# Hybrid attention/convolution layer: places of their own for the first head's weight pieces, loads issued in order of need, sums of squares on VectorE

## The chip, the cores and the metric

The kernel runs on one NeuronCore of a Trainium2 chip. The metric is the device time in microseconds of one execution. Three timed runs of the kernel before gave a median of 2090.63 us (2089.04 to 2090.69). One further execution was profiled; it took 2091.11 us, and the profile covers a span of 2087.8 us of it. All places in time below (for instance "44.2 us") count from the start of that span.

## The reference, cut to what matters

One decoder layer on 512 tokens of width 2048, preceded by 16 meta tokens (528 columns in all), in float32:

```python
n = _rmsnorm(h, g_mix[l])                    # h: 528 x 2048
p = n @ w_in[l]                              # 2048 x 6144: q, k, v, b, c, u
q = _rmsnorm(q.reshape(b, L, 8, 128), g_q)   # 8 heads of 128
k = _rmsnorm(k.reshape(b, L, 8, 128), g_k)
o_attn = _stick_breaking_attention(q, k, v)
o_conv = gb * _causal_dwconv(gc * u, conv_w[l])
o = concat(_rmsnorm(o_attn), _rmsnorm(o_conv))
h = h + o @ w_out[l]
n2 = _rmsnorm(h, g_ffn[l])
h = h + (silu(n2 @ w_gate) * (n2 @ w_up)) @ w_down
```

The root mean square of a token needs all 2048 features of x. The kernel does not wait for it: it multiplies x by the gain only, runs the projections on that, and applies the token's scale `r` to their results.

## The kernel before, in words

Features lie on the 128 partitions, tokens on the free axis. x is 16 tiles `xt` of 128 features by 528 tokens; a weight matrix comes in pieces of 128 rows by a few hundred to 1024 columns. Each operand of a product is split into two parts of a 32-bit matmul type: `hi` (a cast on ScalarE) and `lo` (the rest, a subtraction on VectorE). A tile then takes three matmul passes, hi by hi, hi by lo and lo by hi, on lines 276, 278 and 280 (`product_steps`).

**Stages.** First the eight heads: for each head a product for k, one for q and one for v (`pk`, `pq`, `pv`, 16 tiles each), with the attention of the head before interleaved. Then two convolution channel groups by plain products (`pcu`, `pb`), six by a scheme that needs seven block products for eight (lines 732 to 734), then the output projection, and the feed-forward layer, which fills most of the time.

**The first head** is where the change lies. Its k and q products are built alongside the loading and splitting of x. The list `FIRST` cuts the 16 tiles into groups of 2, 2, 4, 4 and 4. For each group there is one weight piece for k and one for q: ten pieces, four of 256 columns and six of 512. They are the loads 0 to 9; the loads 10 and 11 are the two pieces of v (1024 columns each). For a group the code loads its x tiles (`load_x`, line 341), splits them (`split_x`), runs the group's k and q tiles (`next(step)`), and squares its x tiles (`square_x`). `split_x` makes `nh` (line 348 on ScalarE for the first four tiles and the even ones, line 350 on GpSimd for the odd ones from the fifth) and `nl` (line 351, VectorE). `square_x` writes squares on ScalarE (line 359) and adds them on line 360, for even tiles on GpSimd and for odd tiles on VectorE, into two accumulators.

**Places of the weights.** All raw weights pass through one buffer, `w_buf`, with four places of 1024 columns (`PLACES`). `load_at` issues the next load of the list on SyncE's queue (line 173). When a piece has been split (lines 189 and 190), `done_with` issues the next load into the place that it leaves. So the fifth load waits for the first split, and so on. The split pieces go into `s_buf`, which has three places; splits run two pieces ahead of the product. SyncE's queue works in order: behind a load that waits for a place, the loads of x wait too.

**Order of the other work.** `after(n, work)` registers work that runs n tiles later in the program (`tick`). `x_scale` (line 326: it adds the two accumulators, sums over partitions by a matmul on line 330, and makes `r` and `eps_r2`) is registered 8 tiles before the end of the first head's q product. The norms of k and q (`qk_norm`, its `finish` part) run 8 and 10 tiles into the v product; `attend` starts 11 tiles into the next head's k product. `form_blocks(k)` prepares operands for the later convolution products: it loads four pieces of x (line 413), combines them on VectorE, splits them and stores them to the tensor `fc` (line 422). `form_blocks(0)` to `(6)` run in heads 1 to 7, `form_blocks(7)` at the start of the convolution; line 691 reads `fc` back.

The program is laid out by a planner that keeps the written order where operands are expected to be ready and lets other ready work go ahead where they are not; each engine then runs its own list in order, and waits on semaphores.

Of the kernel before, what the change touches and what calls it, by code (L numbers as in the profile page):

```python
# [10 lines left out]
F32R = mybir.dt.float32r  # L11
AF = mybir.ActivationFunctionType
ALU = mybir.AluOpType
PSUM = bass.MemoryType.PSUM

P = 128
D = 2048
SEQ = 512
META = 16
L = META + SEQ  # L20
HEADS = 8
FF = 5632
KT = D // P
# [10 lines left out]
def hybrid_layer(ctx: ExitStack, tc: tile.TileContext, xT, w_in, w_out, w_gu, w_down, vecs, out):  # L34
# [9 lines left out]
    nc = tc.nc  # L44
    ve, sc, gp, pe = nc.vector, nc.scalar, nc.gpsimd, nc.tensor
# [9 lines left out]
    const = open_pool("const", side="right")  # L55
# [13 lines left out]


    vec = keep.tile([P, 75], F32, name="vec")
    gp.dma_start(vec, vecs)
    sc.preload_act_table_set("natural_log_exp_and_others")
    g_mix, g_ffn = vec[:, 0:16], vec[:, 16:32]
    g_att, g_cnv = vec[:, 32:40], vec[:, 40:48]
# [15 lines left out]
        channel_multiplier=1,  # L91
    )

    carry = const.tile([P, P], F32R, name="carry")
    ve.tensor_copy(carry, later)
    ve.tensor_copy(carry[0:1, :], ones[0:1, :])
    ones_r = keep.tile([P, P], F32R, name="ones_r")
    ve.tensor_copy(ones_r, ones)
    later_r = const.tile([P, P], F32R, name="later_r")
    ve.tensor_copy(later_r, later)  # L100
    gq_s = const.tile([P, 1], F32, name="gq_s")
    ve.tensor_scalar(gq_s, g_q, 1.0 / math.sqrt(P), None, ALU.mult)

# [49 lines left out]
    for n in CHUNKS[1:]:  # L153
        for j in range(KT // 2):
            plan_pair(n, [w_down[2 * j + m, k][:, k0 * P : (k0 + n) * P] for k in range(2) for m in range(2)])
        k0 += n

    quads, sums, split_w, used, loaded = {}, {}, [], [0], [0]

    sixth = next(n for n, (i, _) in enumerate(ents) if i != "raw" and pairs[i][0] == 6)  # L160
# [4 lines left out]
    SUMS = {8: (4096, 5120), 6: (3840, 4608)}  # L165
    n_sums = [1]

    def load_at(place):
        key, n, w = loads[loaded[0]]
        loaded[0] += 1  # L170
        t = w_buf[:, place : place + n * P]
        quads[key] = t, place, n
        nc.sync.dma_start(t.rearrange("p (t c) -> p t c", t=2) if len(w.shape) == 3 else t, w)

    def done_with(key):
        _, place, n = quads[key]
        if loaded[0] < len(loads):
            for p in MOVED[place] if loads[loaded[0]][1] == 6 != n else (place,):
                load_at(p)

# [75 lines left out]
    def after(k_tiles, work):  # L256
        waiting.append([k_tiles, work])
# [60 lines left out]
    H = L // 2  # L318
# [20 lines left out]
    def load_x(k):  # L339
        xts.append(xpool.tile([P, L], F32, tag="xt", name=f"xt{k}"))  # L340
        nc.sync.dma_start(xts[k], xT[k])
# [12 lines left out]
    def square_x(k):  # L354
        if k < 2:
            sc.activation(accs[k], xts[k], AF.Square)
        else:
            s = t512(L, "r", 3)
            sc.activation(s, xts[k], AF.Square)
            (gp, ve)[k % 2].tensor_tensor(accs[k % 2], accs[k % 2], s, ALU.add)  # L360

    pk0 = pp.tile([P, 2, 512], F32, tag="pp", name="pk0")
    pq0 = pp.tile([P, 2, 512], F32, tag="pp", name="pq0")
# [1 line left out]
        product_steps([(pk0[:, 0, :H], 0, H), (pk0[:, 1, :H], H, L)], n_hl, KT),  # L365
        product_steps([(pq0[:, 0, :], META, L)], n_hl, KT),
    ]
    load_at(PLACES[0])
    load_x(0)
    load_at(PLACES[1])  # L370
    for a, b in FIRST:
        for k in range(len(xts), b):
            load_x(k)
        if not a:
            load_at(PLACES[2])
            load_at(PLACES[3])
        for k in range(a, b):
            split_x(k)
        if b == KT:
            for k in range(a, b):  # L380
                square_x(k)
            after(8, x_scale)
        for step in steps:
            next(step)
        if b < KT:
            for k in range(a, b):
                square_x(k)
    xpool.release()


# [17 lines left out]
    def form_blocks(k):  # L408

        x4 = stage.tile([P, 4, CH], F32, tag="x4", name=f"x4_{k}")  # L410
        st = stage.tile([P, 8 * CH], F32R, tag="st", name=f"st4_{k}").rearrange("p (i a t) -> p i a t", i=4, a=2)
        for i, kk in ((0, k), (2, k + 8)):
            nc.sync.dma_start(x4[:, i : i + 2], two(xT[kk][:, C0:]))
        for i, kk in ((0, k), (2, k + 8)):
            sc.activation(x4[:, i : i + 2], x4[:, i : i + 2], AF.Copy, scale=g_mix[:, kk : kk + 1])
        a11, a21, a12, a22 = (x4[:, i] for i in range(4))
        ve.tensor_tensor(a22, a22, a21, ALU.subtract)
        ve.tensor_tensor(a21, a11, a21, ALU.subtract)
        ve.scalar_tensor_tensor(a11, a22, -1.0, a11, ALU.mult, ALU.subtract)
        ve.scalar_tensor_tensor(a12, a11, -1.0, a12, ALU.mult, ALU.subtract)  # L420
        split(st[:, :, 0], st[:, :, 1], x4)
        nc.sync.dma_start(fc[:, :, :, k].bitcast(F32), st.bitcast(F32))
# [11 lines left out]
    def halves(ps, n):  # L434
        return ps[:, :, :n]
# [4 lines left out]
    def qk_norm(ps, g, cols, dst, parts_of, name):  # L440

        raw = t512(L, "e", 2)[:, :cols]
        s = t512(L, "e2", 2)[:, :cols]
        sh = apool.tile([P, L], F32R, tag="sh", name=f"sh_{name}")[:, :cols]
        sl = apool.tile([P, L], F32R, tag="sl", name=f"sl_{name}")[:, :cols]
        cuts = [(0, cols)] if cols == SEQ else [(0, H), (H, L)]
        raw_v, s_v = (raw, s) if cols == SEQ else (two(raw), two(s))  # L450
        sc.activation(s_v, ps, AF.Square)
        sc.activation(raw_v, ps, AF.Copy, scale=g)
        split(sh, sl, s)

        def finish():
            v = t512(L, "v", 2)[:, :cols]
            for a, b in cuts:
                q = small(f"ss_{name}{a}")[:, : b - a]
                pe.matmul(q, ones_r, sh[:, a:b], start=True, stop=False)
                pe.matmul(q, ones_r, sl[:, a:b], start=False, stop=True)  # L460
                ve.scalar_tensor_tensor(
                    v[:, a:b], q, 1.0 / P, eps_r2[:, L - cols + a : L - cols + b], ALU.mult, ALU.add
                )
            y = t512(L, "e2", 2)[:, :cols]
            rsqrt(y, v, cols)
            ve.tensor_tensor(dst, raw, y, ALU.mult)
            hi, lo, n = parts_of
            split(hi, lo, dst[:, :n])

        return finish  # L470
# [3 lines left out]
    def head(h):  # L474

        if h:
            pk = pp.tile([P, 2, 512], F32, tag="pp", name=f"pk{h}")
            product([(pk[:, 0, :H], 0, H), (pk[:, 1, :H], H, L)], n_hl)
        else:
            pk = pk0  # L480
        kn = kns[0]
        kh = apool.tile([P, 384], F32R, tag="kh", name=f"kh{h}")
        kl = apool.tile([P, 384], F32R, tag="kl", name=f"kl{h}")
        after(8, qk_norm(halves(pk, H), g_k, L, kn[:, :L], (kh, kl, 384), f"k{h}"))

        if h:
            pq = pp.tile([P, 2, 512], F32, tag="pp", name=f"pq{h}")
            product([(pq[:, 0, :], META, L)], n_hl)
        else:
            pq = pq0  # L490
        qn = apool.tile([P, SEQ], F32, tag="qn", name=f"qn{h}")
        qh = apool.tile([P, SEQ], F32R, tag="qh", name=f"qh{h}")
        ql = apool.tile([P, SEQ], F32R, tag="ql", name=f"ql{h}")
        after(9 if h else 10, qk_norm(pq[:, 0, :], gq_s, SEQ, qn, (qh, ql, SEQ), f"q{h}"))

        pv = pp.tile([P, 2, 512], F32, tag="pp", name=f"pv{h}")
        product([(pv[:, 0, :H], 0, H), (pv[:, 1, :H], H, L)], n_hl)
        vt = t512(L, "e", 2)
        ve.tensor_tensor(two(vt[:, :L]), halves(pv, H), two(r), ALU.mult)
        after(6 if h else 11, lambda: attend(h, kn, kh, kl, qn, qh, ql, vt))  # L500
# [117 lines left out]
        after(14, lambda: sums(2))  # L618

    for h in range(HEADS):  # L620
        if h:
            after(6, lambda h=h: form_blocks(h - 1))
        head(h)

    def token_scale(acc, dst, count, name, work, eng=ve):
# [40 lines left out]

    for j in range(CONV_FIRST):
        if j == 0:
            after(2, lambda: form_blocks(7))
        c1, c2 = halves_of("e"), halves_of("e2")  # L670
        for c in (c1, c2):
            p = pp.tile([P, 2, 512], F32, tag="pp", name="pcu")
            product([(p[:, 0, :CH], C0, C0 + CH), (p[:, 1, :CH], C0 + CH, L)], n_hl)
            sc.copy(two(c), halves(p, CH))
        y = t512(SEQ, "v", 2)[:, :SEQ]
        conv_taps(j, two(c1), two(c2), y)
        pb = pp.tile([P, 2, 512], F32, tag="pp", name=f"pb{j}")
        product([(pb[:, 0, :], META, L)], n_hl)
        gb = t512(SEQ, "e2", 2)[:, :SEQ]
        sc.copy(gb, pb[:, 0, :])  # L680
        if j == 0:
            assert not waiting
            after(10, scale_a)
            apool.release()
            atmp.release()
            const.release()
            blk_pool = open_pool("blk_pool", side="right")
            blk = blk_pool.tile([P, 3, 2, 8, CH], F32R, name="blk")
            for i, n in ((2, 3), (0, 0), (1, 2)):
                for part in range(2):  # L690
                    gp.dma_start(blk[:, i, part], fc[:, n, part], max_dma_last_dim=4160)
        oh, ol, store = stage_out(f"c{j}")
        conv_out(j, gb, y, oh, ol, t512(SEQ, "e", 2)[:, :SEQ], ve)
        store()
# [493 lines left out]
```

## Time and profile before

| what | number |
|---|---|
| median of three runs | 2090.63 us |
| profiled execution, span of its profile | 2091.11 us, 2087.8 us |
| TensorE busy, share of the span | 2046.0 us, 98% |
| VectorE, ScalarE, GpSimd busy | 1723.3, 1046.5, 414.9 us |
| mean granted TensorE clock | 0.991 |
| first head's k and q on TensorE | from 5.4 to 44.2 us |

In the profile PE is TensorE, DVE VectorE, ACT ScalarE, POOL GpSimd and SP SyncE; a q behind an engine is its queue, in which DMAs are issued and waits are held. A row of the timeline gives a start, a duration, the engine, the line of the kernel, the operation, the tile written and the tiles read, a count, and in brackets the idle time of the engine just before, with what ended it. "xN" merges N neighbouring instructions, so a merged row's duration includes what lies between them. A row of the view by windows gives a stretch, its length, each engine's busy time with its count of instructions, the granted clock of TensorE, the busy share of the 16 DMA engines, and the rate at which they moved data. A row of a group gives line, engine, operation, tiles, shapes and count, then busy time and mean ns of one, then the idle time before them.

### The profile page before, as it was taken

What the parts mean: (1) busy time and instruction counts of PE and PEld (TensorE: products, weight loads), DVE (VectorE), ACT (ScalarE), POOL (GpSimd) and SP (SyncE); (2) the same over time, 40 slices, a digit from 0 to 9 for tenths busy, and PEclk for the clock granted to TensorE, in tenths of its full rate; (3) what the DMA queues carried; (4) which work ended last, traced back from release to release, by engine and by line L of the source; (5) the groups of instructions that cost most, each with busy time, mean ns of one, the idle gap of its engine ahead of it and who ended that gap; (6) DMA issues with size and microseconds to landing.
All of it is one profiled execution on the core that took longest, in us unless ns stands there. A gap on an engine that the chain in (4) does not pass through costs nothing.

```text
span 2087.8 us, 39731 instructions
## 1 busy us (share of the span) xinstructions
PE 2046.0 (98%) x16158; PEld 1979.0 (95%) x16158; DVE 1723.3 (83%) x2186; ACT 1046.5 (50%) x1511; POOL 414.9 (20%) x559
## 2 busy tenths in 40 slices
PE   8999999999999998999999999999999889999999
PEld 6999999999998888999999999999999889999999
DVE  7878877578877778998989989989899867888887
ACT  5666656444443435554555555545555433444443
POOL 3111111220015443111110111111101332223110
PEclk8999999999999999999999999999999989999999
DMA  6343334653356656556554555655555989989864
GB/s 205 107 152 118 121 123 133 219 154 106 103 205 186 183 177 217 153 175 175 163 162 149 169 154 148 173 155 162 164 150 172 300 239 237 262 233 252 242 155 86
DMA packets 161686, 362.21 MB, mean 173 GB/s; under 512 B 13456, under 2 KB 73360, under 8 KB 161504
## 3 DMA queue, kind: packets, MB, share of 16 engines
q1 hardware_dynamic: 78368, 225.80, 34.3%
q0 software_dynamic: 83136, 133.89, 24.4%
q8 instruction: 126, 2.06, 0.4%
q14 instruction: 56, 0.46, 0.1%
HBM read 278.76 MB, written 80.87 MB: 172 GB/s over the span
## 4 chain that ended last, share of the span: by engine, by line
PE 88%; DMA 3%; DVE 3%; issue 2%; ACT 1%; POOL 1%; SPq 0%; DVEq 0%; POOLq 0%; ACTq 0%
PE x L732 12%; PE x L734 12%; PE x L733 12%; PE z L732 6%; PE z L733 6%; PE z L734 6%; PE y L733 3%; PE y L732 3%; PE y L734 3%; PE po L829 3%; PE po L830 3%; PE po L831 3%; PE pv L276 1%; PE pv L278 1%; PE pv L280 1%
## 5 line engine op out<-in xcount | busy, mean ns | idle before, releaser
L189 ACT CAST s_buf<-w_buf 128x1024 fp32r<-128x1024 f32 (+2 forms) x665 | 659.4, 992 | 790.4 <-PE x L733 350.6
L190 DVE TENSOR_TENSOR s_buf<-w_buf,s_buf 128x1024 fp32r<-128x1024 f32 (+2 forms) x665 | 769.8, 1158 | 197.8 <-ACT s_buf L189 196.7
L733 PE MATMUL x<-f,s_buf 128*128 128x256 f32 x1408 | 388.3, 276 | 3.0 <-DMA f<-fx 1.8
L734 PE MATMUL x<-f,s_buf 128*128 128x256 f32 x1408 | 388.1, 276 | 3.0 <-DVE s_buf L190 3.0
L732 PE MATMUL x<-f,s_buf 128*128 128x256 f32 x1408 | 388.1, 276 | 0.2 <-ACT f L290 0.2
L198 DVE TENSOR_TENSOR w_buf<-w_buf 128x1024 f32<-128x1024 f32 (+1 forms) x243 | 278.5, 1146 | 19.0 <-DMA w_buf<-w_in 10.7
L733 PEld LDWEIGHTS x<-f,s_buf 128*128 128x128 f32 x1408 | 265.0, 188 | 3.4 <-DMA f<-fx 2.0
L734 PEld LDWEIGHTS x<-f,s_buf 128*128 128x128 f32 x1408 | 265.1, 188 | 3.2 <-DVE s_buf L190 3.2
L732 PEld LDWEIGHTS x<-f,s_buf 128*128 128x128 f32 x1408 | 265.0, 188 | 0.5 <-ACT f L290 0.4
L1002 POOL DMA_DIRECT2D fd<-s x147 | 103.9, 925 | 690.8 <-DVE s L291 689.2
L732 PE MATMUL z<-f,s_buf 128*128 128x256 f32 x704 | 193.6, 275 | 0.0
L733 PE MATMUL z<-f,s_buf 128*128 128x256 f32 x704 | 193.6, 275 | 0.0
L734 PE MATMUL z<-f,s_buf 128*128 128x256 f32 x704 | 193.6, 275 | 0.0
L732 PE MATMUL x<-ring,s_buf 128*128 128x256 f32 x608 | 168.1, 276 | 4.4 <-DVE d L768 4.4
L734 PE MATMUL x<-ring,s_buf 128*128 128x256 f32 x608 | 168.0, 276 | 1.0 <-DVE s_buf L190 1.0
L733 PE MATMUL x<-ring,s_buf 128*128 128x256 f32 x608 | 168.0, 276 | 0.0
L733 PEld LDWEIGHTS z<-f,s_buf 128*128 128x128 f32 x704 | 132.1, 188 | 0.1
L732 PEld LDWEIGHTS z<-f,s_buf 128*128 128x128 f32 x704 | 132.1, 188 | 0.0
L734 PEld LDWEIGHTS z<-f,s_buf 128*128 128x128 f32 x704 | 132.1, 188 | 0.0
L1068 POOL DMA_DIRECT2D out_T<-d x62 | 60.1, 990 | 326.6 <-DVE d L1074 273.8
L732 PEld LDWEIGHTS x<-ring,s_buf 128*128 128x128 f32 x608 | 114.8, 189 | 4.6 <-DVE d L768 4.6
L734 PEld LDWEIGHTS x<-ring,s_buf 128*128 128x128 f32 x608 | 114.9, 189 | 1.2 <-DVE s_buf L190 1.2
(380 smaller groups left out, 5310.2 us busy)
## 6 DMA issues: line engine op xcount, KB each, us to landing
w_buf<-w_gu SPq DMA_DIRECT2D x176, 512.0 KB, 3.4
w_buf<-w_in SPq DMA_DIRECT2D x92, 512.0 KB, 3.4
fd<-s POOLq DMA_DIRECT2D x147, 256.0 KB, 5.3
w_buf<-w_down SPq DMA_DIRECT2D x96, 384.0 KB, 4.9
ring<-fd POOLq DMA_DIRECT2D x42, 768.0 KB, 8.9
w_buf<-w_out SPq DMA_DIRECT2D x32, 512.0 KB, 3.5
out_T<-d POOLq DMA_DIRECT2D x62, 256.0 KB, 5.4
fc<-st SPq DMA_DIRECT2D x8, 1040.0 KB, 6.2
```

Source lines behind the costliest of these rows:

```text
L189: sc.copy(hi, src)
L190: ve.tensor_tensor(lo, src, hi.bitcast(F32), ALU.subtract)
L198: ve.tensor_tensor(sums[name], a, b, ALU.add)
L276: pe.matmul(ps, wh, ah[:, a:b], start=k == 0, stop=False)
L732: pe.matmul(p, hi[:, kk], act(0, k), start=start and j == k == 0, stop=False, skip_group_check=skip)
L733: pe.matmul(p, hi[:, kk], act(1, k), start=False, stop=False, skip_group_check=skip)
L734: pe.matmul(p, lo[:, kk], act(0, k), start=False, stop=k == n - 1, skip_group_check=skip)
L829: pe.matmul(ps, hi[:, kk], ah, start=k == order[0], stop=False)
L830: pe.matmul(ps, hi[:, kk], al, start=False, stop=False)
L831: pe.matmul(ps, lo[:, kk], ah, start=False, stop=k == order[-1])
L1002: gp.dma_start(fd[c][s][:, :, k], t[:, :, i])
L1068: gp.dma_start(two(out[j]), c, accum_op=ALU.add)
```

## The change

- The small tensor of gains `vec` is loaded through SyncE's queue, as its first load, and no longer through GpSimd's.
- `HEAD_PLACES` gives each of the loads 0 to 11 columns of `w_buf` of its own: the ten pieces of k and q take 0 to 4095, the two of v the columns from 4096 and 5120. All twelve and all 16 x tiles are issued up front. Within a group the order is the piece of k, half of the group's x tiles, the piece of q, the other half.
- Load 12 and those behind it go into the four places: `FREED` issues loads 12 to 15 when pieces 3, 5, 7 and 9 have been split. From load 12 on the rule is that of before.
- The squares of a group come one group later in the program (`late`), the last two groups' behind the last tiles. All their sums are on VectorE.
- `x_scale` is registered behind the first head's k and q, 10 tiles on, so it runs 10 tiles into the v product. The norms of k and q of the first head run 11 and 12 tiles into it.
- The copies that make `later_r` and `carry` (constants of the attention) stand behind this stage.
- `form_blocks` runs one head later: none in head 1, 0 to 5 in heads 2 to 7, 6 and 7 in the first convolution product, at its tiles 2 and 12.

```diff
-    gp.dma_start(vec, vecs)
+    nc.sync.dma_start(vec, vecs)
...
+    EARLY = {loads[i][0]: i for i in range(2 * len(FIRST) + 2)}
...
+    HEAD_PLACES = [sum(2 * (b - a) * P for a, b in FIRST[:i]) + m * (b - a) * P for i, (a, b) in enumerate(FIRST) for m in range(2)]
+    HEAD_PLACES += [4096, 5120]
+    FREED = {3: 0, 5: 1024, 7: 2048, 9: 3072}
...
     def done_with(key):
         _, place, n = quads[key]
-        if loaded[0] < len(loads):
+        if key in EARLY:
+            if EARLY[key] in FREED:
+                load_at(FREED[EARLY[key]])
+        elif loaded[0] < len(loads):
...
-            (gp, ve)[k % 2].tensor_tensor(accs[k % 2], accs[k % 2], s, ALU.add)
+            ve.tensor_tensor(accs[k % 2], accs[k % 2], s, ALU.add)
...
-    load_at(PLACES[0])
-    load_x(0)
-    load_at(PLACES[1])
+    for i, (a, b) in enumerate(FIRST):
+        for m in range(2):
+            load_at(HEAD_PLACES[2 * i + m])
+            for k in range(len(xts), (a + b) // 2 if m == 0 else b):
+                load_x(k)
+    for place in HEAD_PLACES[2 * len(FIRST) :]:
+        load_at(place)
+    limit[0] = 2 * len(FIRST)
+    late = []
     for a, b in FIRST:
-        for k in range(len(xts), b):
-            load_x(k)
-        if not a:
-            load_at(PLACES[2])
-            load_at(PLACES[3])
         for k in range(a, b):
             split_x(k)
         if b == KT:
-            for k in range(a, b):
-                square_x(k)
-            after(8, x_scale)
+            limit[0] = len(ents)
         for step in steps:
             next(step)
-        if b < KT:
-            for k in range(a, b):
-                square_x(k)
+        for k in late:
+            square_x(k)
+        late = range(a, b)
+    for k in late:
+        square_x(k)
+    after(10, x_scale)
...
-        after(8, qk_norm(halves(pk, H), g_k, L, kn[:, :L], (kh, kl, 384), f"k{h}"))
+        after(8 if h else 11, qk_norm(halves(pk, H), g_k, L, kn[:, :L], (kh, kl, 384), f"k{h}"))
...
-        if h:
-            after(6, lambda h=h: form_blocks(h - 1))
+        if h > 1:
+            after(6, lambda h=h: form_blocks(h - 2))
...
-            after(2, lambda: form_blocks(7))
+            after(2, lambda: form_blocks(6))
+            after(12, lambda: form_blocks(7))
```

More of the change, by code (lines that the diff above doesn't have):

```diff
@@ L92, in hybrid_layer @@
     )
-    carry = const.tile([P, P], F32R, name="carry")
-    ve.tensor_copy(carry, later)
-    ve.tensor_copy(carry[0:1, :], ones[0:1, :])
     ones_r = keep.tile([P, P], F32R, name="ones_r")
     ve.tensor_copy(ones_r, ones)
-    later_r = const.tile([P, P], F32R, name="later_r")
-    ve.tensor_copy(later_r, later)
     gq_s = const.tile([P, 1], F32, name="gq_s")
@@ L379, in hybrid_layer @@
         if b == KT:
-            for k in range(a, b):
-                square_x(k)
-            after(8, x_scale)
+            limit[0] = len(ents)
         for step in steps:
             next(step)
-        if b < KT:
-            for k in range(a, b):
-                square_x(k)
+        for k in late:
[4 more added lines that the diff above has]
+    after(10, x_scale)
+    later_r = const.tile([P, P], F32R, name="later_r")
+    ve.tensor_copy(later_r, later)
+    carry = const.tile([P, P], F32R, name="carry")
+    ve.tensor_copy(carry, later)
+    ve.tensor_copy(carry[0:1, :], ones[0:1, :])
     xpool.release()
@@ L493, in head @@
         ql = apool.tile([P, SEQ], F32R, tag="ql", name=f"ql{h}")
-        after(9 if h else 10, qk_norm(pq[:, 0, :], gq_s, SEQ, qn, (qh, ql, SEQ), f"q{h}"))
+        after(9 if h else 12, qk_norm(pq[:, 0, :], gq_s, SEQ, qn, (qh, ql, SEQ), f"q{h}"))
         pv = pp.tile([P, 2, 512], F32, tag="pp", name=f"pv{h}")
```

## The prediction

> **What bounds the kernel now.** The page first: TensorE is busy 98% of the span, and its one visible dip is the first slice of 52 us.
>
> ```profile
> span 2087.8 us, 39731 instructions
> PE 2046.0 (98%) x16158; PEld 1979.0 (95%) x16158; DVE 1723.3 (83%) x2186; ACT 1046.5 (50%) x1511; POOL 414.9 (20%) x559
> PE   8999999999999998999999999999999889999999
> ```
>
> Then the view by windows, cut where the first head changes: its k and q products (to 44.2 us), the gap before v, v and the next head's k up to the end of the first attention scores (70.8 us), a steady stretch, and two steps of 5 us.
>
> ```profile
> 0.00:44.20 44.20, 35.40 (x165) 28.99 (x166) 30.79 (x43) 24.54 (x41) 20.10 (x22) 0.85 0.67 218
> 44.20:46.15 1.95, 1.05 (x5) 0.56 (x3) 1.95 (x3) 1.95 (x4) 0.00 (x0) 1.00 0.02 4
> 46.15:70.80 24.65, 23.93 (x186) 23.00 (x187) 22.65 (x39) 14.15 (x23) 1.74 (x2) 1.00 0.52 165
> 70.80:110.00 39.20, 39.20 (x266) 36.25 (x265) 30.22 (x51) 25.28 (x45) 5.15 (x14) 1.00 0.26 86
> 10.00:15.00 5.00, 4.04 (x15) 3.32 (x16) 2.47 (x7) 2.42 (x5) 1.48 (x1) 0.63 0.86 281
> 15.00:20.00 5.00, 4.08 (x13) 2.84 (x12) 3.78 (x4) 3.90 (x8) 2.51 (x3) 0.50 0.71 232
> ```
>
> From 70.8 us on TensorE has no idle time, so what the first 70 us save or lose reaches the end. In the first 44.2 us it is idle for 8.8 us, and its clock is 0.85 in the mean, 0.63 and 0.50 between 10 and 20 us. The timeline of TensorE tells what the stage needs:
>
> ```profile
> 5.36 0.51 PE L276 MATMUL pk<-nh,s_buf 128*128 128x264 f32 x2
> ...
> 10.21 0.51 PE L276 MATMUL pk<-nh,s_buf 128*128 128x264 f32 x2 [1.35 <-ACT nh L348]
> ...
> 37.00 0.51 PE L276 MATMUL pk<-nh,s_buf 128*128 128x264 f32 x2 [1.80 <-POOL nh L350]
> ...
> 44.20 1.05 PE L330 MATMUL ssx<-acc_x,ones 128*128 128x264 f32 x4
> 46.15 0.51 PE L276 MATMUL pv<-nh,s_buf 128*128 128x264 f32 x2 [0.90 <-ACT tmp L452]
> ...
> 59.83 0.40 PE L276 MATMUL pk<-nh,s_buf 128*128 128x264 f32 x2
> ...
> 67.79 0.60 PE L506 MATMUL va<-ident,tmp 128*128 128x128 f32 x4
> ...
> 69.12 0.50 PE L522 MATMUL z<-ql,kh 128*128 128x512 f32 x1 [0.21 <-DVE ql L291]
> ...
> 74.53 0.39 PE L276 MATMUL pq<-nh,s_buf 128*128 128x512 f32 x1
> ...
> 79.38 0.39 PE L276 MATMUL pq<-nh,s_buf 128*128 128x512 f32 x1
> ```
>
> Between 59.83 and 67.79 lie 11 k tiles: 0.724 us a tile. Between 74.53 and 79.38 lie 7 q tiles: 0.693 us. So 16 tiles of both need 16 x 1.417 = **22.7 us** at full clock. The stage takes 44.2 - 5.4 = 38.8. Of the 16.1 us above need, the clock takes 0.15 x 35.40 = 5.3, and 10.8 are waiting and refilling.
>
> Why are operands late? SyncE's waits up to 38 us, its timeline, and the DMA issues up to 75 us:
>
> ```profile
> SPq L173 <- DVE s_buf L190: 20.8, 9, 5.5
> ...
> 18.13 1.85 SPq L341 DMA_DIRECT2D xt<-xT  x4
> ...
> 33.81 0.56 SPq L341 DMA_DIRECT2D xt<-xT  x1
> ...
> xt<-xT SPq DMA_DIRECT2D x16, 264.0 KB, 4.4
> w_buf<-w_in SPq DMA_DIRECT2D x6, 256.0 KB, 3.9
> w_buf<-w_in SPq DMA_DIRECT2D x4, 128.0 KB, 3.0
> ```
>
> SyncE stands for 20.8 us until a split frees a place, and the x loads stand behind it: the last xt is issued at 33.8 us and lands some 4 us later. Split, product and load form a ring that turns at the speed of its slowest member.
>
> **The change part by part.**
>
> *Loads (places, order, `vec` on SyncE).* Nothing in the first head waits for a place any more. An issue takes 0.43 us (1.85 / 4), so the 27 issues up to the last xt take about 12 us; transfer is what remains. Its volume is 16 x 264 + 6 x 256 + 4 x 128 KB = 6272 KB, and 37.5 KB of `vec`: 6.46 MB. The rates at hand:
>
> ```profile
> 2.00:16.90 14.90, 12.39 (x54) 9.62 (x53) 6.99 (x15) 8.27 (x17) 2.76 (x6) 0.81 0.84 270
> 60.00:65.00 5.00, 5.00 (x43) 5.00 (x43) 4.82 (x8) 2.75 (x4) 0.00 (x0) 1.00 0.97 338
> ```
>
> At 270 GB/s it takes 23.9 us, at 338 GB/s 19.1; from 2.0 us, and with about 1 us until the landing is seen (an estimate), the last xt is there between 22 and 27 us. I take 24.5. Even at 270 GB/s a tile takes about 1.5 us against TensorE's 1.42, so loading is at worst level with the products. `vec` goes ahead of the rest and costs piece 0 and the first xt one issue, 0.4 us; `vec` itself is issued earlier by its place in front. I count nothing either way (bounds -0.5 and +0.5).
>
> *VectorE.* The groups up to 44.2 us:
>
> ```profile
> L351 DVE SCALAR_TENSOR_TENSOR nl<-xt,vec,nh 128x528 fp32r<-128x528 f32 x16 | 18.3, 1171 | 3.0 <-ACT nh L348 2.3 <-POOL nh L350 0.6
> L360 POOL TENSOR_TENSOR acc_x<-acc_x,tmp 128x528 f32<-128x528 f32 x7 | 10.5, 1494 | 13.3 <-ACT tmp L359 13.3
> L350 POOL TENSOR_SCALAR nh<-xt,vec 128x528 fp32r<-128x528 f32 x6 | 8.0, 1329 | 5.0 <-DMA xt<-xT 5.0
> L360 DVE TENSOR_TENSOR acc_x<-acc_x,tmp 128x528 f32<-128x528 f32 x7 | 4.9, 698 | 0.1
> L190 DVE TENSOR_TENSOR s_buf<-w_buf,s_buf 128x512 fp32r<-128x512 f32 x6 | 4.2, 708 | 2.8 <-ACT s_buf L189 2.7
> L190 DVE TENSOR_TENSOR s_buf<-w_buf,s_buf 128x256 fp32r<-128x256 f32 x4 | 1.7, 422 | 0.9 <-ACT s_buf L189 0.9
> ...
> L351 DVE SCALAR_TENSOR_TENSOR nl<-xt,vec,nh x16: 751/946/1860, 5.3 to 40.5; 128x528 fp32r<-128x528 f32 x16
> ```
>
> Seven sums move from GpSimd to VectorE: +7 x 0.70 = 4.9 us there, -10.5 us on GpSimd. An `nl` takes 0.75 us at least and 1.17 on average; the long ones lie beside GpSimd's sums, so without them I take 0.75 (bounds 0.75 and 1.17). The program puts six sums (tiles 2 to 7) ahead of the last `nl`. VectorE then needs, before that `nl` is done, 16 x 0.75 + 4.2 + 1.7 + 6 x 0.70 = 22.1 us; started at 4.7 us it is done at 26.8 at the earliest. With `nl` at 1.17 it would be 33.5. The other eight sums lie under TensorE's remaining tiles and the v product.
>
> *TensorE, to the end of q.* From 5.4 us, 22.7 us of work: 28.1. VectorE comes to almost the same (26.8, then the last tile's remaining passes, 1.0 us). Two engines equally loaded never mesh without idle time: today's named waits for operands are 2.8 + 2.8 + 1.8 = 7.4 us, as the waits of TensorE have it:
>
> ```profile
> PE pk L276 <- ACT nh L348: 2.8, 3, 1.4
> PE pk L278 <- DVE nl L351: 2.8, 6, 0.7
> PE pk L276 <- POOL nh L350: 1.8, 1, 1.8
> ```
>
> I take a third or so, 2.7 us (bounds 0 and 7.4): the end of q at **30.8** for 44.2. The clock term goes to 0 in this.
>
> That last point hangs on a mechanism. The row at 10.21 shows 1.35 us of idle time, and the window from 10 us a clock of 0.63, so here a gap that short went with the fall. The Trainium skill (TensorE: Matmul & The Clock Gate, Part 1) has the clock go to half only after an idle window of about 3.4 us. No idle time of that length stands in these rows, so the trace does not bear the rule out as worded. By the rule the clock cannot fall in the changed stage; by the row it can, and that is the first rival below.
>
> *From q to v.* The v product needs the PSUM place of k, which ScalarE must have read (lines 451, 452). Today 1.95 us pass, 1.05 of them filled by the matmuls of `x_scale`, which now come later. I take 1.3 us (bounds 0.7 and 1.95).
>
> *x_scale later.* Its matmuls start 10 x 0.724 = 7.2 us into v, and add their 1.05 us to the stretch from v to the end of the scores. Today `z` finds its `ql` 69.12 - 44.2 = 24.9 us after them. TensorE reaches `z` some 16 x 0.724 + 1.05 + 1.0 (the sums of the norms) + 11 x 0.724 + 0.9 = 22.5 us into v. Kept at 24.9, the data would come at 32.1, 9.6 us late. But `form_blocks(0)` has left this stretch (3.4 us of VectorE: 1.71 for its split of 1040 columns, row below, and as much, by estimate, for four combinations of 260 each), and the squares of k and q are split ahead (2 x 0.70, as for a sum of that width): 27.3. Of the 4.8 missing, the five k tiles that follow can fill 3.6 (5 x 0.724). I take **+1.2** (bounds 0 and 9.6).
>
> ```profile
> 53.82 1.71 DVE L291 TENSOR_TENSOR st<-x,st 128x1040 fp32r<-128x1040 f32 x1
> 350.00:390.00 40.00, 40.00 (x290) 38.04 (x289) 29.34 (x45) 22.01 (x36) 6.07 (x15) 1.00 0.35 115
> 395.30 4.35 POOL L691 DMA_DIRECT2D blk<-fc  x6 [0.30 <-POOL acc_a L310]
> ```
>
> *form_blocks one head later.* The first convolution product now holds two. TensorE is at 40.00 of 40.00 us there, VectorE has 10.7 us free for the additional 3.4 us or so, and the last store must land before `blk` is read at 395.3 us, about 30 us after tile 12 of that product. Nothing; without that cover, a few us. The copies of `carry` and `later_r` (0.2 us each) count nothing.
>
> **The sum.** 30.8 + 1.3 + (24.65 + 1.05 + 1.2) = 59.0 us for 70.8: **11.8 us less**. The profiled execution took 2091.11, which gives 2079.3; it lies 0.48 above the median of the runs, so the timed runs should show **2078.8**. With terms at their likely ends the forecast's own range is 2075 to 2082.
>
> **Rivals.**
>
> *The clock falls again* (0.18). If 1.35 us of idle time is enough, the start, where each tile waits for its own xt, can do it again. For: the row at 10.21. Against: x2 and x3 no longer stand behind a place. Price: today's 5.3 us, so 2084.1.
>
> *The scale is late* (0.10). The planner keeps `z` where it is written, and TensorE waits the whole 4.8, and 1.4 more where ScalarE is late too, 5 us above what I took: 2083.8. For: the sum above is short before any filling. Against: today's `z` waits only 0.21 us.
>
> *The loads come no sooner* (0.05): something else than the places holds SyncE or the transfers back. For: a rate of 270 GB/s while several loads stood ready. Against: the four x loads issued in 1.85 us. Time: 2090.6.
>
> *Half clock throughout, slower than before* (0.05). If loads now meter the products tile by tile, with a short gap in every stretch of a few us, the clock stays at 0.5 over the whole stage: 2 x 22.7 + 5.4 + 2.7 = 53.5 instead of 30.8, 22.7 later, 2101.5. It decides once gaps as small as those between 15 and 20 us, where TensorE was busy 4.08 of 5.00 us and the clock stayed down, recur up to the end. Against: loading at 1.5 us a tile or better is twice as fast as products at half clock (2.83), so TensorE would build up a backlog and lose the gaps.
>
> **How the numbers follow.** The forecast itself has 0.62. Its range and the two rivals of reduced gain make the range 2074.5 to 2086; no change and slower lie outside, with what little of the rivals exceeds it. A measurement of this kernel can tell 0.2%, 4.2 us, from no change: forecast, fallen clock and late scale all gain more, 0.90; 0.05 within; 0.05 slower.
>
> **What would show it.** Right: no waits of SyncE for `s_buf` before 20 us; the last xt issued near 12 us and landed by 27; `nl` near 0.75 us and no sums on GpSimd; a granted clock of 1.00 in the windows from 10 to 30 us; the `ssx` matmuls within the v product; the first `pv` at 32 us for 46.15, and the end of the first scores near 59. Wrong: `pv` later than 38 us, a clock of 0.5 in more than one window, a wait of `z` of several us, or TensorE idle in the first convolution product.

## The result, and the profile after

Timed side by side, the changed kernel took 2080.32 us (2078.78 to 2085.0, 4 runs) and the kernel before 2090.66 (2089.04 to 2091.67, 4 runs): the medians lie 10.3 us apart. The ratio of the runs is 0.9941, 95% interval 0.9916 to 0.9965; it is not the quotient of the medians, which is 0.9951. The forecast was 2078.8. The direction, the range and nearly the size are right. The way to it is not, as the profile shows; its execution took 2085.0 us.

The page of the changed kernel, its span, busy times and slices:

```profile
span 2083.2 us, 39726 instructions
PE 2044.4 (98%) x16158; PEld 1978.6 (95%) x16158; DVE 1719.8 (83%) x2193; ACT 1045.9 (50%) x1511; POOL 403.7 (19%) x551
...
PE   9999999999999999999999999999999879999999
```

The dip of the first slice is gone. The view by windows, cut at the first `pv`, at the first q product of the second head, and in steps of 5 us:

```profile
0.00:37.23 37.23, 32.50 (x164) 27.03 (x165) 28.55 (x48) 24.33 (x41) 10.08 (x14) 0.95 0.81 271
37.23:65.57 28.34, 28.19 (x221) 27.41 (x221) 24.14 (x39) 15.61 (x24) 1.87 (x2) 1.00 0.24 78
350.00:390.00 40.00, 39.31 (x267) 36.30 (x266) 26.24 (x44) 22.88 (x38) 9.90 (x20) 1.00 0.52 165
...
10.00:15.00 5.00, 4.82 (x31) 4.02 (x31) 5.00 (x9) 4.34 (x8) 1.54 (x1) 1.00 0.75 270
15.00:20.00 5.00, 4.15 (x23) 3.14 (x21) 4.96 (x11) 2.04 (x4) 1.37 (x1) 1.00 0.81 264
20.00:25.00 5.00, 2.88 (x15) 2.28 (x15) 3.22 (x6) 4.18 (x7) 1.53 (x2) 0.91 0.88 320
25.00:30.00 5.00, 5.00 (x24) 4.38 (x23) 4.48 (x7) 2.02 (x4) 2.77 (x2) 0.75 0.80 240
```

The first `pv` starts at 37.2 us: 8.9 us sooner than before (46.15), but 5 later than the 32.1 of the forecast. From there to the second head's q product it is 28.34 us; before it was 74.53 - 46.15 = 28.38. Between 20 and 25 us TensorE is busy 2.88 of 5.00 us, and then runs at a clock of 0.75 in the mean. SyncE's timeline tells why:

```profile
5.52 0.90 SPq L344 DMA_DIRECT2D xt<-xT  x2
6.88 3.70 SPq L173 DMA_DIRECT2D w_buf<-w_in  x2
10.62 0.91 SPq L344 DMA_DIRECT2D xt<-xT  x2
14.48 0.80 SPq L173 DMA_DIRECT2D w_buf<-w_in  x2
15.33 0.90 SPq L344 DMA_DIRECT2D xt<-xT  x2
...
18.24 1.05 SPq L344 DMA_DIRECT2D xt<-xT  x2
24.96 0.81 SPq L173 DMA_DIRECT2D w_buf<-w_in  x2
25.80 0.91 SPq L344 DMA_DIRECT2D xt<-xT  x2
```

Its waits up to 38 us, and TensorE's up to 45 us:

```profile
SPq L173 <- DVE s_buf L193: 10.5, 4, 3.4
SPq L173 <- DMA w_buf<-w_in: 6.1, 3, 3.3
...
PE pk L281 <- DVE nl L354: 1.9, 5, 0.8
PE pk L279 <- ACT nh L351: 1.5, 1, 1.5
```

SyncE still stands for splits, at 10, 14 and 25 us, and the last two xt are issued at 25.8 us and landed at 32.3. These waits are not those of the ten pieces. They belong to loads 12 to 15, which `done_with` issues into the columns that pieces 3, 5, 7 and 9 leave (`FREED`). `prepare`, which calls it, runs under `tc.high_priority()`, so the planner lays these loads into SyncE's list ahead of the x loads that are written before them. With p for the pieces, the list from the tenth load on is: p4, x4, x5, p5, load 12, x6, x7, load 13, p6, x8, x9, p7, x10, x11, p8, x12, x13, load 14, p9, x14, x15. Loads 12, 13 and 14 each wait for a split, and what the first head needs next waits behind them. (The view puts part of these stands down to landings of pieces, the 6.1 us above; in e1 below, where the order is another, that entry is 0.3 us.)

The groups of VectorE up to 38 us:

```profile
L354 DVE SCALAR_TENSOR_TENSOR nl<-xt,vec,nh 128x528 fp32r<-128x528 f32 x16 | 12.7, 808 | 5.4 <-ACT nh L351 3.7 <-POOL nh L353 1.7
L363 DVE TENSOR_TENSOR acc_x<-acc_x,tmp 128x528 f32<-128x528 f32 x14 | 9.2, 697 | 0.0
```

`nl` takes 0.808 us for 1.171, and a sum 0.697, both much as forecast.

### The profile page after: what moved, and what is told of

It reads as the page before. It is cut to its first block, busy times and chain, and to the rows that moved or that the text cites. A ratio compares the mean times of both kernels' runs of the same rounds, so it can differ in the third digit from the quotient of the medians.

```text
span 2083.2 us, 39726 instructions
## 1 busy us (share of the span) xinstructions
PE 2044.4 (98%) x16158; PEld 1978.6 (95%) x16158; DVE 1719.8 (83%) x2193; ACT 1045.9 (50%) x1511; POOL 403.7 (19%) x551
## 3 DMA queue, kind: packets, MB, share of 16 engines
q0 software_dynamic: 83104, 133.85, 24.6%
## 4 chain that ended last, share of the span: by engine, by line
PE 87%; DMA 4%; DVE 4%; issue 2%; ACT 2%; POOL 1%; SPq 0%; DVEq 0%; POOLq 0%; ACTq 0%
PE x L745 12%; PE x L744 12%; PE x L743 12%; PE z L743 6%; PE z L744 6%; PE z L745 6%; PE y L744 3%; PE y L743 3%; PE y L745 3%; PE po L842 2%; PE po L840 2%; PE po L841 2%; PE pv L279 2%; PE pv L281 1%; PE pv L283 1%
## 6 DMA issues: line engine op xcount, KB each, us to landing
w_buf<-w_down SPq DMA_DIRECT2D x96, 384.0 KB, 4.9
```

## The experiments

All profiles in one table: the first `pv` and the first block product `y` of the convolution, in us from the span's start, and the rest of the span behind `y`. The ratio is that of the runs to those of the kernel before, timed beside it, with its interval. Kernels run twice or three times have a row for each.

| kernel | pv | y | y to end | median us (runs) | ratio |
|---|---|---|---|---|---|
| before | 46.2 | 429.4 | 1658.4 | 2090.66 (4) | 1 |
| changed | 37.2 | 421.0 | 1662.2 | 2080.32 (4) | 0.9941 [0.9916, 0.9965] |
| changed, a2 | 35.9 | 419.6 | 1656.9 | 2086.26 (10) | 0.9955 [0.9938, 0.9972] |
| changed, a3 | 36.1 | 420.1 | 1661.9 | 2082.4 (6) | 0.9954 [0.9936, 0.9971] |
| e1 | 32.6 | 416.7 | 1656.7 | 2081.36 (6) | 0.9939 [0.9923, 0.9955] |
| e1 again | 32.5 | 416.8 | 1668.8 | 2083.73 (6) | 0.9941 [0.9921, 0.9962] |
| e1 third | 32.8 | 418.0 | 1657.2 | 2079.88 (5) | 0.9941 [0.9927, 0.9955] |
| e2 | 40.4 | 424.6 | 1662.8 | 2091.83 (10) | 0.9987 [0.9974, 1.0] |
| e3 | 36.6 | 422.4 | 1661.2 | 2083.98 (4) | 0.9952 [0.9936, 0.9968] |
| e4 | 40.5 | 426.8 | 1664.9 | 2087.89 (9) | 0.9963 [0.9948, 0.9978] |
| e5 | 40.6 | 424.4 | 1662.6 | 2090.61 (10) | 0.9986 [0.9968, 1.0003] |
| e6 | 32.8 | 419.7 | 1665.5 | 2081.81 (6) | 0.9953 [0.9936, 0.9969] |
| e7 | 35.0 | 419.9 | 1664.9 | 2082.98 (4) | 0.9935 [0.991, 0.996] |

The column "y to end" is to be read first. Behind `y` all kernels run the same program, yet one execution differs from another by up to 12 us, e1 against e1 as well. So the places of `pv` and `y` tell causes apart, and the times only with several runs. The median of the kernel before, timed beside them, was 2095.12 us for e1 to e4, 2094.54 for a2, e1 again, e5 and e7, and 2092.5 for a3, e1 third and e6.

**e1: the freed loads behind the x loads.** The changed kernel, in which loads 12 to 15 are issued at ordinary priority:

```diff
 def prepare():
     i, s = ents[len(split_w)]
+    if (i, s) in EARLY:
+        with tc.high_priority():
+            split_quad(quads[i, s][0], loads[s][1])
+        done_with((i, s))
+        return
     with tc.high_priority():
```

> The changed kernel, with one thing altered: the loads 12 to 15, which the splits of pieces 3, 5, 7 and 9 release, stand behind all loads of x and of the first twelve pieces in SyncE's list, instead of among them. Theory A (in the changed kernel SyncE still holds loads of x back, because a released load waits ahead of them; its trace shows xt loads issued only at 25.8 and 26.3 us behind an issue at 24.96): SyncE has no wait for a split before about 13 us, the last xt is issued by 14 us and lands by 27, no gap of TensorE above 1 us between 6 us and the end of q, no window at half clock, first pv at 31 to 33 us instead of 37.2, time 4 to 6 us below the changed kernel, about 2075. Theory B (the transfers themselves or VectorE's work are what limits the changed stage): first pv within 1 us of 37.2, time within 1.5 us of the changed kernel's 2080.3.

> The kernel of e1_freed_behind again, beside the changed kernel. Its two profiles have the first y block at 416.7 and 416.8 us, those of the changed kernel at 421.0 and 419.6. If what the first head gains reaches the end, it is 3 to 4 us faster than the changed kernel in the median (0.15 to 0.2%); if the waits of the last 440 us take it back, the medians agree within 1 us.

The timeline of SyncE in e1's third profile, and its waits up to 38 us:

```profile
14.98 1.02 SPq L349 DMA_DIRECT2D xt<-xT  x2
16.34 10.77 SPq L173 DMA_DIRECT2D w_buf<-w_in  x6
...
SPq L173 <- DVE s_buf L193: 14.5, 3, 7.2
SPq L173 <- DMA xt<-xT: 2.7, 8, 0.5
SPq L349 <- DMA xt<-xT: 1.4, 5, 0.3
SPq L349 <- DMA w_buf<-w_in: 1.3, 4, 0.3
```

The same execution by windows, and its group of `nl`:

```profile
10.00:15.00 5.00, 4.83 (x31) 4.05 (x30) 5.00 (x8) 4.42 (x8) 3.33 (x2) 1.00 1.03 381
15.00:20.00 5.00, 4.42 (x28) 3.65 (x27) 5.00 (x7) 3.32 (x6) 3.60 (x3) 1.00 1.05 398
20.00:25.00 5.00, 4.69 (x30) 3.97 (x29) 5.00 (x8) 2.19 (x5) 2.03 (x3) 1.00 1.04 412
...
L359 DVE SCALAR_TENSOR_TENSOR nl<-xt,vec,nh 128x528 fp32r<-128x528 f32 x16 | 13.3, 861 | 2.1 <-ACT nh L356 2.1
```

No x load waits for a split now: the 14.5 us of such waits lie behind the last of them, in the row from 16.34 us. The last xt is issued by 16.0 us and landed at 21.1, data move at 381 to 412 GB/s between 10 and 25 us for 264 to 320, and `pv` comes at 32.5 to 32.8 us, where the forecast had put it (32.1). VectorE is busy 5.00 of 5.00 us from 10 us on, so it may be what sets the pace now; no run shows that (e7 below was meant to and did not relieve it). The order of the queue is thus shown to be what kept the changed kernel from its forecast, worth 3 to 5 us at `pv`. At `y` it is 3 us in the mean (417.2 for 420.2). In time, the two comparisons in which both kernels were timed side by side (a2 with e1 again, a3 with e1 third) give 1.8 +- 2.0 and 2.9 +- 1.5 us for e1 (difference of the means and its standard error), weighted 2.5 +- 1.2. That is less than the 3 to 6 us expected: e1 is probably the better kernel, at the edge of what these runs can tell.

> The changed kernel itself, beside its variants on one chip. Both theories: first pv within 1 us of 37.2, first pq of the second head within 1 us of 65.6, time 8 to 12 us below the kernel before, with runs spread over some 6 us as before.

> The changed kernel a third time. Its clock fell once in the first head in one profile of two. If the fall hangs on where 1.5 us of waits come to lie, its first y block is at 419.5 to 421.5 us again, with or without a fall; SyncE stands for splits between 10 and 25 us in each execution, whatever the clock does. Against before 0.994 to 0.996.

> The version with the released loads behind the others, again, on the same chip as the changed kernel. Theory A (the gain of 4.6 us at the first pv reaches the end): 3 to 6 us below the changed kernel in the median. Theory B (it is given back later, where the clock falls between 1640 and 1760 us): within 1.5 us of the changed kernel though its first pv is again 4 to 5 us earlier.

The changed kernel again gave `pv` at 35.9 and 36.1 us, with the clock at 1.00 throughout, for 37.2 with a stretch of half clock. So the fall cost some 1.2 us, if nothing else differs between the three executions, and the order of the queue the rest.

**e2: the even sums back on GpSimd, in e1.**

```diff
-    ve.tensor_tensor(accs[k % 2], accs[k % 2], s, ALU.add)
+    (gp, ve)[k % 2].tensor_tensor(accs[k % 2], accs[k % 2], s, ALU.add)
```

> As the run with the released loads behind, and the sums of squares of the even tiles back on GpSimd as in the kernel before. Theory A (GpSimd's sums lengthen the nl operations beside them, and VectorE is nearly as loaded as TensorE once the loads are free): mean nl 1.0 us or more for about 0.77, first pv 1 to 3 us later than with all sums on VectorE. Theory B (VectorE has room, where the sums stand does not matter): first pv within 0.7 us of that run.

Its groups up to 45 us, its largest wait of TensorE, and a window:

```profile
L359 DVE SCALAR_TENSOR_TENSOR nl<-xt,vec,nh 128x528 fp32r<-128x528 f32 x16 | 17.3, 1106 | 4.4 <-ACT nh L356 2.5 <-POOL nh L358 1.9
L368 POOL TENSOR_TENSOR acc_x<-acc_x,tmp 128x528 f32<-128x528 f32 x7 | 14.9, 2134 | 12.2 <-ACT tmp L367 12.0
...
PE pk L286 <- DVE nl L359: 6.4, 4, 2.4
...
20.00:25.00 5.00, 3.70 (x14) 3.22 (x15) 5.00 (x5) 3.94 (x7) 5.00 (x4) 0.66 1.03 409
```

With all loads in time, GpSimd's seven sums alone take `nl` from 0.86 to 1.11 us and `pv` from 32.6 to 40.4: 7.8 us, where 1 to 3 were expected of it. A stretch of 3.41 us at half clock (0.66 in this window) is part of that, 1.7 us at most, and so is an `nh` on GpSimd that comes late behind its sums (1.9 us of VectorE's waits). It is `nl` that grows; of GpSimd's sums one takes 5.58 us and the other six 1.31 to 1.77, as all seven did before (1.32 to 1.77), so that their mean of 2134 ns rests on that one. The Trainium skill (SBUF — State Buffer, Who interferes with whom) says "only the shared port pair causes contention, and it's an exclusive lock", of VectorE and GpSimd; the trace agrees in that `nl` grows beside GpSimd's sums, and no run here shows the lock itself.

**e4: the places alone**, on the kernel before: `HEAD_PLACES`, `FREED`, the order of the loads (the freed loads ahead, as in the changed kernel) and `vec`, with sums, `late`, `x_scale`, the norms and `form_blocks` as before. **e5: all the rest alone**, with the loads as before. One thing is in neither: the changed kernel's `limit`, which holds the splits of v back until the last group of tiles.

```diff
e4, against before
-    gp.dma_start(vec, vecs)
+    nc.sync.dma_start(vec, vecs)
...
+        if key in EARLY:
+            if EARLY[key] in FREED:
+                load_at(FREED[EARLY[key]])
e5, against the changed kernel
+    load_at(PLACES[0])
+    load_x(0)
+    load_at(PLACES[1])
```

> The kernel before with the places, the order of the loads and the gains through SyncE alone; squares, sums, scale, norms and form_blocks as before. Theory A (the loads carry most of the gain): first pv at 37 to 40 us, time 6 to 9 us below the kernel before. Theory B (without the squares one group later and the sums off GpSimd the loads bring little): first pv above 43 us, time less than 3 us below the kernel before.

> The kernel before with everything of the change but the places, the order of the loads and the gains through SyncE: squares one group later, all sums on VectorE, the copies, the scale, the norms and form_blocks later. Theory A (the loads wait for splits as before, and this is what holds the first head): first pv above 42 us, xt loads still behind waits of SyncE up to 30 us, time within 4 us of the kernel before. Theory B (GpSimd's sums were what made the splits slow, so that without them the ring of split and load turns faster): first pv at 38 to 42 us, time 4 to 8 us below the kernel before.

TensorE's waits up to 45 us and the group of `nl` in e4, and then TensorE's and SyncE's waits in e5:

```profile
PE pk L286 <- DVE nl L359: 7.1, 9, 1.3
...
L359 DVE SCALAR_TENSOR_TENSOR nl<-xt,vec,nh 128x528 fp32r<-128x528 f32 x16 | 17.6, 1117 | 4.3 <-ACT nh L356 2.7 <-POOL nh L358 1.6
```

```profile
PE pk L271 <- ACT nh L343: 3.3, 3, 1.4
PE pk L273 <- DVE nl L346: 2.7, 3, 1.2
...
SPq L168 <- DVE s_buf L185: 17.8, 9, 4.2
```

Each part alone leaves the other limit standing: `nl` at 1.117 us in e4, nine waits of SyncE for splits in e5. `pv` comes at 40.5 and 40.6, in e4 a little behind the 37 to 40 expected. For e5 the expectations split: the place fits the theory that GpSimd's sums slowed the ring, the time the one that the waits for splits hold the first head.

How much each part gains depends on the clock of the kernel before. Its 46.2 holds 5.3 us of half clock, as the forecast worked out, and neither e4 nor e5 has any. With all of that taken off (40.9), each part alone would gain next to nothing at `pv` and both together 5. But the fall in the changed kernel cost less than its own time, and no profile shows before without a fall, so it may stand anywhere between 40.9 and 46.2. As measured, each alone gains 5.6 us at `pv`, both together 8.9 to 10.3, and 13.4 to 13.7 with the queue in order (e1). At `y` e4 gains 2.6 and e5 5.0 us, 7.6 in sum, and both together 8.4 to 9.8, so there the parts nearly add up. In time e4 gains 0.37% and e5 0.14%, whose interval holds no change. How often before's clock falls in its other executions no profile shows, so how much of e4's gain is the clock stays open, and whether the two parts need each other as well.

**e3: the scale early.** The changed kernel with `x_scale` and the norms nearer to their places of before:

```diff
-after(10, x_scale)
+after(1, x_scale)
-    after(8 if h else 11, qk_norm(halves(pk, H), ...
+    after(8, qk_norm(halves(pk, H), ...
-    after(9 if h else 12, qk_norm(pq[:, 0, :], ...
+    after(9 if h else 10, qk_norm(pq[:, 0, :], ...
```

> The changed kernel with the scale of x 1 tile into the v product instead of 10, and the norms of k and q at 8 and 10 tiles as before instead of 11 and 12. Theory A (the later scale costs nothing, since the planner fills the wait for the scores with later tiles, and it keeps the matmuls of the scale out of the way of v's start): the stretch from the first pv to the first pq of the second head stays at 28.3 us or grows by up to 1 us; time within 1.5 us of the changed kernel. Theory B (the later scale costs 1 us or more, as the prediction had it): the stretch shrinks by 1 us or more and the time with it.

`pv` stays (36.6). From there to the second head's q product it is 28.85 us, for 28.30 to 28.34 in the changed kernel's three profiles, and to `y` 385.8 for 383.8 to 384.0. The later scale costs nothing, and may save 2 us; one profile of e3 stands for this.

**e6: `form_blocks` as before, in e1.**

```diff
-    if h > 1:
-        after(6, lambda h=h: form_blocks(h - 2))
+    if h:
+        after(6, lambda h=h: form_blocks(h - 1))
```

> The kernel of e1_freed_behind, with the blocks of a head's correction formed one head after it again, as before the change: form_blocks(0) lies between the first v product and the first scores once more, and the first convolution product holds one form_blocks, not two. If the move is worth nothing because other work hides it (as predicted): the first pv stays at 32.5 us, and from there to the first y block stay 384.1 to 384.3 us. If VectorE's 3.4 us there are on the path (rival): the first scores come 1 to 3.4 us later, and the way from pv to y is 385 to 388 us. In both cases no stall at the convolution product.

From `pv` to `y` it takes 386.9 us, for 384.1 to 385.2 in e1. The first transposes of the attention start 24.6 us behind `pv` instead of 21.8, and the last stretch, from the eighth head's transposes to `y`, is 1.0 us shorter (70.9 for 71.9). So `form_blocks(0)` did lie on the path of the first scores, as the rival had it: its move saves 2.8 us there and costs 1.0 in the convolution product. One profile of e6 stands for this.

**e7: all squares behind the last tiles, in e1**, which was to take six sums off VectorE ahead of the last `nl`.

```diff
-        for k in late:
-            square_x(k)
-        late = range(a, b)
-    for k in late:
+    for k in range(KT):
         square_x(k)
```

> As the version with the released loads behind, and all squares written behind the last tiles of the first head's q instead of one group later. Theory A (with the loads free VectorE, busy 5.00 of 5.00 us from 10 to 35 us, sets the pace, and the sums of tiles 2 to 7, 6 x 0.70 = 4.2 us, stand ahead of the last nl): first pv 1.5 to 3 us earlier than 32.6, the scores of the first head later, the first pq of the second head 0 to 3 us earlier. Theory B (the planner had them in idle stretches already): first pv within 0.7 us of 32.6.

VectorE's sums up to 27.5 us in e1's third profile and in e7, then the timeline of e7 at the first `pv`:

```profile
L368 DVE TENSOR_TENSOR acc_x<-acc_x,tmp 128x528 f32<-128x528 f32 x6 | 5.0, 838 | 0.0
...
L368 DVE TENSOR_TENSOR acc_x<-acc_x,tmp 128x528 f32<-128x528 f32 x5 | 4.3, 870 | 0.0
...
33.09 1.32 ACT L367 ACTIVATE tmp<-xt 128x528 f32<-128x528 f32 x2
34.31 0.68 ACT L464 ACTIVATE tmp<-pk,vec 128x528 f32<-128x528 f32 x1
...
35.05 0.56 PE L284 MATMUL pv<-nh,s_buf 128*128 128x264 f32 x2 [3.00 <-ACT tmp L464]
```

The planner laid the sums nearly where they are in e1: five stand ahead of the last `nl`, for six. So e7 did not relieve VectorE, and what its load is worth in e1 stays untested. The k and q products end at 32.05 us, as in e1 (32.0 to 32.3), and then TensorE stands for 3.00 us: in e7 three squares and a cast of weights go ahead of ScalarE's second read of k (line 464), which ends at 35.0 us and frees the place of v; in e1 one square does, and that read starts at 32.0 us. `pv` comes 2.4 us later than in e1, where 1.5 to 3 sooner had been expected.

**Where equal programs differ.** TensorE's waits between 1640 and 1770 us and that stretch as a window, in e1 again and then in e1 third:

```profile
PE z L748 <- ACT d L776: 19.5, 3, 9.0
...
1640.00:1770.00 130.00, 104.94 (x831) 103.78 (x830) 86.66 (x110) 43.88 (x56) 47.12 (x44) 0.88 0.86 227
```

```profile
PE z L748 <- ACT d L776: 12.7, 3, 5.5
...
1640.00:1770.00 130.00, 110.99 (x908) 109.84 (x907) 93.20 (x120) 47.99 (x62) 40.07 (x47) 0.93 0.91 246
```

The same program stood 6.8 us longer here in one execution than in the other, and its clock was 0.88 for 0.93 in the mean. This is likely to be part of why the profiled execution of the changed kernel took 2085.0 us and its median is 2080.32: its three such waits came to 16.1 us, a2's to 14.4. It is not the only such place: a3, with 14.3, took 5.0 us longer behind `y` than a2, and there the difference lies between 800 and 1000 us (TensorE busy 196.01 us at a clock of 0.98, for 198.44 at 1.00).

## Why the prediction was right, and where it was wrong

**Loads: wrong, and the step that failed.** "Nothing in the first head waits for a place any more" holds for loads 0 to 11 only. "The 27 issues up to the last xt take about 12 us" became 26.7, since three freed loads stood in between, each held for its place; the last xt landed at 32.3 us where 24.5 was taken, with 27 as the bound. Even in e1 the issues take until 16.0 us: the short waits for the landing of earlier loads (2.7, 1.4 and 1.3 us above) were not in the sum, and 1.85 / 4 is 0.46 us from issue to issue, not 0.43. The bounds of the rate, 270 and 338 GB/s, were both too low: they came from stretches in which the issues stalled, and loads issued without a long stall moved at up to 412.

**VectorE: right.** `nl` went to 0.808 us (0.75 taken, bounds 0.75 and 1.17), 0.861 in e1's third profile, the sums to 0.697 (0.70). Left at 1.17, the forecast's sum would have been 6.7 us longer (33.5 for 26.8); e2 measured 7.8, up to 1.7 of it half clock.

**Idle time of TensorE: 3.4 us** of named waits (1.9 and 1.5) where 2.7 was taken, and 1.0 in e1's third profile.

**Clock: partly wrong.** Taken as 0, it was (1 - 0.95) x 32.50 = 1.6 us in one profile of three, and cost only some 1.2 at `pv`, probably because the loads set the pace there. One execution of three stands for this. The rival priced it at 5.3.

**From q to v: 1.3 taken, 0 measured** (the last `pq` starts at 37.0, `pv` at 37.23), 0.5 in e1, 3.0 in e7. The mechanism named, ScalarE's read of k's PSUM place, is the one that e7 shows.

**Scale: +2.25 taken, 0 measured** (28.34 us for 28.38). Of the 1.05 us of `ssx`, 0.57 went into idle time (24.65 - 23.93 = 0.72 us before, 28.34 - 28.19 = 0.15 now); these rows do not show where the rest went. The planner set `z` among and behind the last k tiles, so that the whole shortage was filled and not three quarters of it. For the same reason the end of the first scores, forecast near 59, came at 65.6 us: k tiles that used to follow now go ahead of it.

**`form_blocks`: nothing taken at its new place, some 1.0 us measured** by e6; TensorE is idle for 0.69 us in the window from 350 to 390 us, where it was busy throughout before. The 2.8 us that its move saves ahead of the scores, by e6, are part of why the scale cost nothing.

**The sum: nearly right, by errors that cancel in part, which is luck.** The first `pv` came 5.1 us later than forecast (37.2 for 32.1, a q to v that was 1.3 better within), the stretch behind it was 2.3 shorter: 11.8 - 5.1 + 2.3 = 9.0. At the second head's q product the gain is indeed 74.53 - 65.57 = 9.0 us, at `y` 8.4 to 9.8, between the medians 8.3 to 10.3, for 11.8. In e1, where the loads nearly do what the forecast said of them, `y` gains 11.4 to 12.8 and the medians 10.8 to 13.8 us. The rivals: the falling clock came once, at a quarter of its price (1.2 for 5.3); the late scale and half clock throughout did not come; "the loads come no sooner" came in part (the last xt was issued at 26.3 us, for 33.8 before and 12 forecast), by a mechanism that it left unnamed.

## What to carry to other kernels

When loads get places of their own, look at the whole list that the issuing queue will run, and not only at the loads that were given places: one load that still waits for a place, laid ahead by a priority, holds everything behind it. One limit can take back what the removal of another gave: with the loads in order, the sums on GpSimd alone took back 7.8 of the 13.6 us that e1 gained at `pv`. Before a part's own gain is quoted, see that the kernel beside it ran at the same clock, and that the planner laid the work where the change meant it to lie. Where the tail of a kernel varies by more than the change is worth, compare places in the trace ahead of that tail, over two or three executions.

## What the runs showed of the hardware that was not expected

The clock fell after less idle time than expected and not always. In the changed kernel's timeline, and in windows of 3.41 us:

```profile
21.59 0.51 PE L279 MATMUL pk<-nh,s_buf 128*128 128x264 f32 x2 [1.54 <-ACT nh L351]
22.39 0.51 PE L281 MATMUL pk<-nl,s_buf 128*128 128x264 f32 x2 [0.29 <-DVE nl L354]
...
23.77 0.52 PE L281 MATMUL pk<-nl,s_buf 128*128 128x264 f32 x2 [0.29 <-DVE nl L354]
...
20.72:24.13 3.41, 1.95 (x11) 1.51 (x12) 1.95 (x3) 3.31 (x6) 0.92 (x1) 1.00 1.01 382
24.13:27.54 3.41, 3.41 (x14) 2.95 (x13) 2.89 (x6) 2.24 (x4) 2.90 (x2) 0.50 0.56 162
```

Three gaps of 2.1 us together within 3.7 us, and from 24.13 to 27.54 us TensorE ran at half clock, 3.41 us long. In e5 gaps of 1.40, 0.71, 1.18 and 0.74 us between 9.5 and 19.1 us left it at 1.00. The traces tell much of what decides. In each of the thirteen profiles every stretch between two changes of the clock lasts a whole multiple of 3.413 us, so the changes lie on a grid. Cut on that grid, 81 of the 83 falls follow a piece in which TensorE was busy for 0.44 of the time or less, and no piece at full clock that was busy for so little goes without one. Above 0.58 none falls. In between both occur: 0.57 (the 1.95 of 3.41 us above) and 0.55 (the first fall of the kernel before) were followed by a fall, 0.51 in e5 (from 37.76 us) was not. The four gaps in e5 lie in pieces that were busy for 0.64 and more. So it appears to be the busy share of one piece of the grid that decides, and a gap would count for less when it is split between two pieces. Where the limit lies between 0.44 and 0.58 these traces do not tell, since the ends of matmuls are modelled. The Trainium skill (TensorE: Matmul & The Clock Gate, Part 1) asks for an idle window of about 3.4 us; the length of the slow stretch agrees, but no idle time of that length stands ahead of this one.
